# Split-precision projections: high and low activation parts in one 512-column matmul

## The chip, the cores and the metric

The kernel runs on one core of a Trainium2 chip. The metric is device time in microseconds, from the first to the last work of one execution; three timed runs give a median.

## The reference

Two transformer blocks over 256 tokens of 1024 features, float32. Block 1 has two layers, each a SwiGLU feed-forward, a mixer and another SwiGLU feed-forward; block 2 has a mixer of attention and a recurrence, and a convolutional gated feed-forward. Cut to what matters here:

```
def swiglu(h, w_gate, w_up, w_down):          # 1024 -> 2816 -> 1024
    return (jax.nn.silu(h @ w_gate) * (h @ w_up)) @ w_down

for layer in range(2):
    x = x + 0.5 * swiglu(rms_norm(x, ffn1_norm[layer]), ...)
    h = rms_norm(x, mix_norm[layer])
    x = x + (even_mixer(h, ...) if layer == 0 else odd_mixer(h, ...))
    x = x + 0.5 * swiglu(rms_norm(x, ffn2_norm[layer]), ...)
x = rms_norm(x, final_norm)
...                                           # block 2: mixer, gated feed-forward
```

Almost all of the arithmetic is the product of an activation map with a weight matrix.

## The kernel before

**Split products.** Every operand of a projection is split into a high part (rounded to the short float32 format that TensorE takes at full rate) and a low part (the rest). A product is three matmuls into the same place of a PSUM bank: high by high, high weight by low activation, low weight by high activation (`mm3`, lines 301 to 305). The weight tile, 128x128, is the loaded side, and the 256 tokens are the 256 columns that stream. `mm3n` (lines 327 to 331) is the other form, activations loaded and 256 or 512 weight columns streaming; the change leaves it alone.

**Weights.** They come from memory in blocks of 128x1024, eight weight tiles each, on SyncE's queue. `prep` makes the two parts: ScalarE writes `wh` (line 288), VectorE subtracts for `wl` (line 290; some blocks on GpSimd). There are five buffers of each, and `block` keeps six blocks in preparation.

**Activations.** `xh` and `xl` hold eight tiles of 256 tokens, four tiles to a slot of 1024 columns: high parts in two slots, low parts in two others. The feed-forward's inner map (`hh`, `hl`) takes six and six slots for its 22 tiles, the mixers' outputs (`oh`, `ol`) two and two. The pool has 23 slots, given out in turn.

**Stages.** ffn10, mix0, ffn20, ffn11, mix1, ffn21 (block 1), mix2, ffn2 (block 2). A feed-forward of block 1 (`ffn`, lines 450 to 490) runs an up phase over 22 tiles of the inner map: gate block, up block, then VectorE multiplies the gate's bank by the token factor (line 464), ScalarE applies SiLU (466), VectorE multiplies by the up bank (468), and the product is split (469, 470). A down phase follows: 8 output tiles of 22 weight tiles each, then lines 484 and 486, and the next norm's split (`norm_tile`, 383 and 384). The output projections of the mixers are in `out_half`: 8 tiles of four products per half, one VectorE add to `x` each (line 1410 or 1412). In mix2 the second half also makes the split map of the next norm (`def_tile`, 921 and 922), for projections that start before its statistics are known (`def_proj`). `proj_t_steps` serves the query and key projections of mix1 (lines 790 to 806) and mix2 (`main`).

**Order.** The order of the instructions on each engine is set by a scheduler that simulates the program when it is built; the generators only give it the program's order. Banks: four named `mm`, two `sc` (`six_ps` uses all six where attention doesn't), two `aux`.

## Time and profile before

| | us |
|---|---|
| three timed runs | 1420.96, 1419.38, 1416.65; median 1419.38 |
| span of the profiled execution | 1416.2 |
| TensorE, VectorE, ScalarE, GpSimd busy | 1372.7, 942.6, 752.8, 306.0 |

The profiled execution has no time of its own beside its span; the median of the runs is 3.2 us above the span. A matmul's row gives its latency, and matmuls overlap, so what one costs in a stream is the distance between two starts. A weight load (PEld) runs beside the matmul before it. "Idle before, releaser" says how long an engine stood still ahead of an instruction and which instruction ended that.

### The profile page before, as it was taken

To read this page: it belongs to the slowest core of one execution; us is meant where nothing else is said; L and a number is where in the kernel's file an instruction comes from. 1 tells how busy PE (TensorE), PEld (TensorE's weight loads), DVE (VectorE), ACT (ScalarE), POOL (GpSimd) and SP (SyncE) were. 2 spreads that over 40 slices of the span, in tenths; PEclk is the share of its full clock that TensorE was granted. 3 is DMA by queue.
4 is the path that set the end of the run, shared out by engine and by line. 5 is a ranking of instruction groups with operands and counts; after the bars stand their busy time and mean duration, and the time that the engine had idled before them with its cause. 6 is when DMAs were issued, how large, how long until landed. Compare 5 with 4: busy or idle time off the path is not lost.

```text
span 1416.2 us, 26083 instructions
## 1 busy us (share of the span) xinstructions
PE 1372.7 (97%) x10278; PEld 1292.6 (91%) x10278; DVE 942.6 (67%) x1621; ACT 752.8 (53%) x1299; POOL 306.0 (22%) x363
## 2 busy tenths in 40 slices
PE   7999998899999999999999999999989999899997
PEld 6999996579999999999988789999987888799987
DVE  6666656747666656665547766666777778797754
ACT  5444445655444445444467645445557447576642
POOL 4000145423000210000233340000252213741101
PEclk9999999799999999999999999999999999799999
DMA  7655665015555555656565335566546404355561
GB/s 252 190 180 182 185 198 173 8 60 179 181 183 188 180 180 180 188 182 180 186 229 169 101 108 191 181 187 184 180 134 220 132 21 150 118 168 187 182 212 56
DMA packets 64266, 231.70 MB, mean 164 GB/s; under 512 B 7240, under 2 KB 7376, under 8 KB 64144
## 3 DMA queue, kind: packets, MB, share of 16 engines
q1 hardware_dynamic: 61632, 221.41, 49.7%
q0 software_dynamic: 2512, 8.64, 1.7%
q8 instruction: 80, 1.31, 0.4%
q14 instruction: 42, 0.34, 0.1%
HBM read 228.96 MB, written 1.06 MB: 162 GB/s over the span
## 4 chain that ended last, share of the span: by engine, by line
PE 90%; DVE 5%; POOL 2%; ACT 1%; issue 1%; DMA 0%; DVEq 0%; SPq 0%; ACTq 0%
PE mm L303 19%; PE mm L304 18%; PE mm L305 18%; PE sc L304 5%; PE sc L305 5%; PE sc L303 5%; PE mm L331 4%; PE mm L329 4%; PE mm L330 4%; PE mm L549 2%; DVE wl L290 1%; POOL acc L390 1%; PE aux L542 1%; PE sc L518 1%; POOL sq L387 1%
## 5 line engine op out<-in xcount | busy, mean ns | idle before, releaser
L288 ACT ACTIVATE wh<-raw 128x1024 fp32r<-128x1024 f32 (+1 forms) x425 | 443.3, 1045 | 521.3 <-issue 257.3
L290 DVE TENSOR_TENSOR wl<-raw,wh 128x1024 fp32r<-128x1024 f32 (+1 forms) x406 | 510.5, 1260 | 264.8 <-ACT wh L288 263.2
L303 PE MATMUL mm<-xh,wh 128*128 128x256 f32 x1328 | 380.3, 287 | 7.0 <-ACT xh L383 6.0
L304 PE MATMUL mm<-xl,wh 128*128 128x256 f32 x1328 | 380.2, 287 | 3.5 <-DVE xl L384 3.3
L305 PE MATMUL mm<-xh,wl 128*128 128x256 f32 x1328 | 378.5, 285 | 0.3 <-DVE wl L290 0.3
L303 PEld LDWEIGHTS mm<-xh,wh 128*128 128x128 f32 x1328 | 256.7, 194 | 11.0 <-ACT xh L383 6.0
L304 PEld LDWEIGHTS mm<-xl,wh 128*128 128x128 f32 x1328 | 256.6, 193 | 7.3 <-DVE xl L384 5.6
L305 PEld LDWEIGHTS mm<-xh,wl 128*128 128x128 f32 x1328 | 256.8, 193 | 1.4 <-DVE wl L290 0.8
L303 PE MATMUL mm<-hh,wh 128*128 128x256 f32 x704 | 199.2, 283 | 0.0
L304 PE MATMUL mm<-hl,wh 128*128 128x256 f32 x704 | 199.2, 283 | 0.0
L305 PE MATMUL mm<-hh,wl 128*128 128x256 f32 x704 | 199.2, 283 | 0.0
L303 PE MATMUL sc<-xh,wh 128*128 128x256 f32 x560 | 158.7, 284 | 1.9 <-DVE wgb L942 1.9
L304 PE MATMUL sc<-xl,wh 128*128 128x256 f32 x560 | 159.1, 284 | 0.0
L305 PE MATMUL sc<-xh,wl 128*128 128x256 f32 x560 | 158.8, 284 | 0.0
L387 POOL TENSOR_TENSOR sq<-xt 128x256 f32<-128x256 f32 x48 | 36.6, 765 | 514.8 <-DVE xt L486 471.4
L303 PEld LDWEIGHTS mm<-hh,wh 128*128 128x128 f32 x704 | 135.2, 192 | 0.0
L304 PEld LDWEIGHTS mm<-hl,wh 128*128 128x128 f32 x704 | 135.2, 192 | 0.0
L305 PEld LDWEIGHTS mm<-hh,wl 128*128 128x128 f32 x704 | 135.2, 192 | 0.0
L303 PEld LDWEIGHTS sc<-xh,wh 128*128 128x128 f32 x560 | 107.7, 193 | 2.1 <-ACT xt L898 2.1
L305 PEld LDWEIGHTS sc<-xh,wl 128*128 128x128 f32 x560 | 107.7, 192 | 0.1
L304 PEld LDWEIGHTS sc<-xl,wh 128*128 128x128 f32 x560 | 107.6, 192 | 0.1
L331 PE MATMUL mm<-wh,xl 128*128 128x512 f32 x144 | 56.9, 403 | 2.6 <-DVE xl L900 2.6
(345 smaller groups left out, 2265.2 us busy)
## 6 DMA issues: line engine op xcount, KB each, us to landing
raw<-wst SPq DMA_DIRECT2D x417, 512.0 KB, 3.6
m1b<-m1bias POOLq DMA_DIRECT2D x8, 512.0 KB, 4.9
xt<-xT SPq DMA_DIRECT2D x4, 256.0 KB, 5.3
patf<-m2pat POOLq DMA_DIRECT2D x2, 512.0 KB, 6.4
kb<-scr POOLq DMA_DIRECT2D x2, 512.0 KB, 5.9
out<-x2n SPq DMA_DIRECT2D x4, 256.0 KB, 2.0
raw<-wst SPq DMA_DIRECT2D x2, 256.0 KB, 4.2
m0tab<-m0tab POOLq DMA_DIRECT2D x1, 512.0 KB, 3.8
```

Source lines behind the costliest of these rows:

```text
L288: self.nc.scalar.activation(wh[:, c], r[:, c], AF.Copy)
L290: e.tensor_tensor(out=wl[:, c], in0=r[:, c], in1=wh[:, c].bitcast(F32), op=ALU.subtract)
L303: mm(ps, wh, xh, start=first, stop=False)
L304: mm(ps, wh, xl, start=False, stop=False)
L305: mm(ps, wl, xh, start=False, stop=last)
L329: mm(ps, xh, wh, start=first, stop=False)
L330: mm(ps, xh, wl, start=False, stop=False)
L331: mm(ps, xl, wh, start=False, stop=last)
L387: nc.gpsimd.tensor_tensor(out=sq, in0=self.x(j), in1=self.x(j), op=ALU.mult)
L390: self.last_acc = nc.gpsimd.tensor_tensor(out=acc, in0=sq, in1=self.acc, op=ALU.add)
L518: self.nc.tensor.matmul(ps[:, qt], q[own, h, c], low[own], start=False, stop=True)
L549: self.nc.tensor.matmul(po[half * 64:half * 64 + 64, :T], v[kt], pT[:, kt], start=kt == 0, stop=kt == 1)
```

## The change

Each activation tile's high and low parts now lie side by side, 512 columns, two tiles to a slot. `mm2` takes the place of `mm3` where a whole bank is free: one 512-column matmul of the high weight with both parts (high sums in the first half of the bank, low in the second), and one 256-column matmul of the low weight with the high part into the first half. The two halves are then added: `fold` copies the second half out with ScalarE, and VectorE adds the first. The first operation that used the bank before now takes the folded tile. In `out_half` the two halves go to `x` in two VectorE operations; in mix2 the copy was there already, so only an add is new. `ffn2` still passes a slice of 256 columns to `proj_t`, which keeps `mm3` for it; `def_proj` and `mm3n` are as they were. The rest of the diff drops comments and renames.

```
+    def mm2(self, ps, wh, wl, x2, first, last):
+        mm = self.nc.tensor.matmul
+        if first:
+            mm(ps, wh, x2, start=True, stop=False)
+        mm(ps[:, :T], wl, x2[:, :T], start=False, stop=False, skip_group_check=True)
+        if not first:
+            mm(ps, wh, x2, start=False, stop=last)
...
     def proj_t(self, ps):
...
-            self.mm3(ps, wh[:, s], wl[:, s], self.xh(k), self.xl(k), k == 0, k == KD - 1)
+            if ps.shape[1] == 2 * T:
+                self.mm2(ps, wh[:, s], wl[:, s], self.x2(k), k == 0, k == KD - 1)
+            else:
+                self.mm3(ps, wh[:, s], wl[:, s], self.xh(k), self.xl(k), k == 0, k == KD - 1)
...
+    def hi(t, k):
+        return t[k // 2][:, (k % 2) * 2 * T:(k % 2) * 2 * T + T]
+    def lo(t, k):
+        return t[k // 2][:, (k % 2) * 2 * T + T:(k % 2 + 1) * 2 * T]
+    def both(t, k):
+        return t[k // 2][:, (k % 2) * 2 * T:(k % 2 + 1) * 2 * T]
...
     def norm_begin(self):
-        self.xht = [self.slot(f"xh{i}", F32R) for i in range(2)]
-        self.xlt = [self.slot(f"xl{i}", F32R) for i in range(2)]
+        self.xs = [self.slot(f"xs{i}", F32R) for i in range(KD // 2)]
...
     def ffn(self, next_gain):
-        hh = [self.slot(f"hh{i}", F32R) for i in range(6)]
-        hl = [self.slot(f"hl{i}", F32R) for i in range(6)]
+        h2 = [self.slot(f"h{i}", F32R) for i in range(KF // 2)]
...
-            pg = self.six_ps()[:, :T]
+            pg = self.six_ps()
...
-            nc.vector.tensor_tensor(out=s, in0=pg, in1=self.rb, op=ALU.mult)
+            self.fold(s, pg)
+            nc.vector.tensor_tensor(out=s, in0=s, in1=self.rb, op=ALU.mult)
...
-            nc.vector.tensor_tensor(out=hp, in0=pu, in1=sg, op=ALU.mult)
+            self.fold(hp, pu)
+            nc.vector.tensor_tensor(out=hp, in0=hp, in1=sg, op=ALU.mult)
...
-                self.mm3(ps, wh[:, s], wl[:, s], h(hh, k), h(hl, k), k == 0, k == KF - 1)
+                self.mm2(ps, wh[:, s], wl[:, s], self.both(h2, k), k == 0, k == KF - 1)
...
-            nc.vector.scalar_tensor_tensor(out=t, in0=ps, scalar=0.5, in1=self.rb,
+            self.fold(t, ps)
+            nc.vector.scalar_tensor_tensor(out=t, in0=t, scalar=0.5, in1=self.rb,
...
+    def fold(self, out, ps):
+        self.nc.scalar.activation(out, ps[:, T:], AF.Copy)
+        self.nc.vector.tensor_tensor(out=out, in0=ps[:, :T], in1=out, op=ALU.add)
...
     def mix1(self, next_gain):      # qkproj, for q; k in the same way
-                nc.vector.scalar_tensor_tensor(out=q, in0=pq, scalar=0.125, in1=self.rb,
+                self.fold(q, pq)
+                nc.vector.scalar_tensor_tensor(out=q, in0=q, scalar=0.125, in1=self.rb,
...
     def mix2(self, first):          # main
-                nc.scalar.activation(dst[:, t], ps, AF.Copy, scale=sc)
+                nc.scalar.activation(dst[:, t], ps[:, T:], AF.Copy, scale=sc)
+                nc.vector.scalar_tensor_tensor(out=dst[:, t], in0=ps[:, :T], scalar=sc, in1=dst[:, t],
+                                               op0=ALU.mult, op1=ALU.add)
...
     def out_half(self, o2, half, gain, alpha=None, ln=False, six=False):
-                self.mm3(ps, wh[:, s], wl[:, s], oh(4 * half + k), ol(4 * half + k), k == 0, k == 3)
+                self.mm2(ps, wh[:, s], wl[:, s], self.both(o2, 4 * half + k), k == 0, k == 3)
...
-                nc.vector.tensor_tensor(out=x, in0=ps, in1=x, op=ALU.add)
+                nc.vector.tensor_tensor(out=x, in0=ps[:, T:], in1=x, op=ALU.add)
+            nc.vector.tensor_tensor(out=x, in0=ps[:, :T], in1=x, op=ALU.add)
```

What this makes of the instructions, at three places. First TensorE, in the first projection of ffn10: two weight tiles before (`xh`, `xl` are the slots of the high and low parts).

```order
L303 MATMUL mm<-xh_108,wh 128x256
L304 MATMUL mm<-xl_110,wh 128x256
L305 MATMUL mm<-xh_108,wl 128x256
L303 MATMUL mm<-xh_109,wh 128x256
L304 MATMUL mm<-xl_111,wh 128x256
L305 MATMUL mm<-xh_109,wl 128x256
```

And the first three weight tiles now (`xs` holds both parts side by side).

```order
L305 MATMUL mm<-xs_108,wh 128x512
L306 MATMUL mm<-xs_108,wl 128x256 x2
L308 MATMUL mm<-xs_108,wh 128x512
L306 MATMUL mm<-xs_109,wl 128x256
L308 MATMUL mm<-xs_109,wh 128x512
```

Three matmuls per tile have become two, one of them twice as wide, and short and long ones alternate.

Second VectorE, in the up phase of a feed-forward of block 1 (`s` is the gate, `hp` the product, `wl` a weight block's low part). Before, one tile of the inner map:

```order
L464 TENSOR_TENSOR s<-mm,rb 128x256
L290 TENSOR_TENSOR wl<-raw,wh 128x1024
L468 TENSOR_TENSOR hp<-mm,sg 128x256
L290 TENSOR_TENSOR wl<-raw,wh 128x1024
L470 TENSOR_TENSOR hl_186<-hp,hh_180 128x256
```

Now:

```order
L522 TENSOR_TENSOR s<-mm,s 128x256
L496 TENSOR_TENSOR h_5131<-hp,h_5131 128x256
L489 TENSOR_TENSOR s<-s,rb 128x256
L290 TENSOR_TENSOR wl<-raw,wh 128x1024
L522 TENSOR_TENSOR hp<-mm,hp 128x256
L494 TENSOR_TENSOR hp<-hp,sg 128x256
L290 TENSOR_TENSOR wl<-raw,wh 128x1024
```

Two adds (line 522) have come in, each ahead of a weight subtraction; each needs a ScalarE copy of the bank's second half.

Third VectorE, in the second half of mix2's output projection (`dl` is the low part of the next norm's map). Before:

```order
L1412 TENSOR_TENSOR xt<-mm,xt 128x256 x4
L290 TENSOR_TENSOR wl<-raw,wh 128x1024
L922 SCALAR_TENSOR_TENSOR dl_13975<-xt,cols,dh_13972 128x256
L1412 TENSOR_TENSOR xt<-mm,xt 128x256
L290 TENSOR_TENSOR wl<-raw,wh 128x1024
```

Now:

```order
L1440 TENSOR_TENSOR xt<-mm,xt 128x256 x3
L1441 TENSOR_TENSOR xt<-mm,xt 128x256 x3
L290 TENSOR_TENSOR wl<-raw,wh 128x1024
L1440 TENSOR_TENSOR xt<-mm,xt 128x256
L952 SCALAR_TENSOR_TENSOR dl_12017<-xt,cols,dh_12014 128x256
L1440 TENSOR_TENSOR xt<-mm,xt 128x256
L290 TENSOR_TENSOR wl<-raw,wh 128x1024
L1441 TENSOR_TENSOR xt<-mm,xt 128x256
```

Each add to `xt` has become two, in the same queue as the weight subtractions and the splits.

## Rows read from the trace of the kernel before

**Rows 1.** The page: the span, busy time and share of each engine with the number of instructions, and the chain of waits by engine and by line.

```profile
span 1416.2 us, 26083 instructions
...
PE 1372.7 (97%) x10278; PEld 1292.6 (91%) x10278; DVE 942.6 (67%) x1621; ACT 752.8 (53%) x1299; POOL 306.0 (22%) x363
...
PE 90%; DVE 5%; POOL 2%; ACT 1%; issue 1%; DMA 0%; DVEq 0%; SPq 0%; ACTq 0%
PE mm L303 19%; PE mm L304 18%; PE mm L305 18%; PE sc L304 5%; PE sc L305 5%; PE sc L303 5%; PE mm L331 4%; PE mm L329 4%; PE mm L330 4%; PE mm L549 2%; DVE wl L290 1%; POOL acc L390 1%; PE aux L542 1%; PE sc L518 1%; POOL sq L387 1%
```

**Rows 2.** Who waited for whom: total us, times, longest us. One row of ScalarE over the whole span, TensorE's four largest over the whole span, and last TensorE's in the window from 8 to 18 us.

```profile
ACT wh L288 <- PE mm L304: 178.5, 116, 4.1
...
PE sc L515 <- ACT p L525: 6.2, 3, 4.9
PE mm L303 <- ACT xh L383: 6.0, 1, 6.0
PE mm L304 <- DVE dl L922: 5.1, 5, 1.9
PE mm L304 <- DVE xl L384: 3.3, 4, 2.0
...
PE mm L304 <- DVE xl L384: 2.9, 3, 2.0
```

**Rows 3.** TensorE's instructions in order of time, in the up phase of ffn10: start us, latency us. First and last of 25 matmuls of 256 columns that follow one another (24 distances).

```profile
100.06 0.28 PE L303 MATMUL sc<-xh,wh 128*128 128x256 f32 x1
...
102.94 0.28 PE L303 MATMUL mm<-xh,wh 128*128 128x256 f32 x1
```

**Rows 4.** The same view in a projection of mix0: first and last of 17 matmuls of 512 columns (16 distances).

```profile
208.00 0.39 PE L329 MATMUL mm<-wh,xh 128*128 128x512 f32 x1
...
211.63 0.39 PE L330 MATMUL mm<-wl,xh 128*128 128x512 f32 x1
```

**Rows 5.** Groups of TensorE's instructions by line and shape, the first line of `mm3`: count, then busy us and mean latency in ns, then idle time before. `mm` and `sc` are banks; `xh`, `hh`, `oh` the activations' high parts.

```profile
L303 PE MATMUL mm<-xh,wh 128*128 128x256 f32 x1328 | 380.3, 287 | 7.0 <-ACT xh L383 6.0 <-ACT wh L288 0.8 <-ACT xh L899 0.2
L303 PE MATMUL mm<-hh,wh 128*128 128x256 f32 x704 | 199.2, 283 | 0.0
L303 PE MATMUL sc<-xh,wh 128*128 128x256 f32 x560 | 158.7, 284 | 1.9 <-DVE wgb L942 1.9
L303 PE MATMUL mm<-oh,wh 128*128 128x256 f32 x184 | 51.3, 291 | 0.0
L303 PE MATMUL sc<-oh,wh 128*128 128x256 f32 x8 | 2.3, 283 | 0.0
```

**Rows 6.** Durations. Groups by line and shape: ScalarE's weight copy, VectorE's weight subtraction and two products that read a bank (mean ns after the busy us). Last, from the view of one tile, ScalarE's copy of 128x256 out of a bank (min/median/max ns).

```profile
L288 ACT ACTIVATE wh<-raw 128x1024 fp32r<-128x1024 f32 x417 | 441.4, 1059 | 518.4 <-issue 257.3 <-PE mm L304 178.5 <-PE mm L331 54.1
L290 DVE TENSOR_TENSOR wl<-raw,wh 128x1024 fp32r<-128x1024 f32 x398 | 506.5, 1274 | 263.1 <-ACT wh L288 261.5
L468 DVE TENSOR_TENSOR hp<-mm,sg 128x256 f32<-128x256 f32 x59 | 25.0, 424 | 34.6 <-PE mm L305 32.9 <-ACT sg L466 1.7
L1412 DVE TENSOR_TENSOR xt<-mm,xt 128x256 f32<-128x256 f32 x40 | 16.0, 417 | 20.9 <-PE mm L305 20.9
...
L553 ACT ACTIVATE oh<-mm x16: 384/384/388, 266.1 to 831.4; 128x256 fp32r<-128x256 f32 x16
```

**Rows 7.** TensorE's instructions in order of time at the end of block 1, where the granted clock fell: first and last of 11 matmuls of 258 columns (10 distances).

```profile
1041.20 0.42 PE L303 MATMUL mm<-dh,wh 128*128 128x258 f32 x1
...
1043.35 0.42 PE L304 MATMUL mm<-dl,wh 128*128 128x258 f32 x1
```

**Rows 8.** Busy us (and instructions) of each engine by stretch, then granted clock as a share of 2.4 GHz, DMA share, GB/s. The columns: stretch, its length, PE, PEld, DVE, ACT, POOL. Four up phases; a projection of mix0; the query and key projections of mix1 with its attention; the end of mix0's and of mix1's output projection.

```profile
13.00:142.00 129.00, 128.56 (x1042) 127.64 (x1041) 84.44 (x118) 63.64 (x97) 6.84 (x13) 1.00 0.61 193
331.00:460.00 129.00, 128.81 (x1072) 128.55 (x1071) 81.27 (x112) 66.00 (x98) 2.17 (x5) 1.00 0.58 186
524.00:652.00 128.00, 128.00 (x1067) 127.95 (x1067) 81.07 (x113) 64.06 (x94) 1.30 (x4) 1.00 0.60 186
850.00:975.00 125.00, 124.81 (x1039) 124.56 (x1038) 80.09 (x122) 64.78 (x97) 2.31 (x6) 1.00 0.59 185
...
206.60:245.00 38.40, 36.22 (x170) 29.29 (x168) 25.93 (x37) 19.95 (x31) 20.75 (x22) 1.00 0.54 168
...
750.00:815.00 65.00, 65.00 (x409) 51.46 (x408) 49.77 (x137) 43.72 (x111) 21.44 (x19) 1.00 0.38 124
...
320.00:331.00 11.00, 10.95 (x91) 10.75 (x90) 10.39 (x15) 4.54 (x8) 10.53 (x12) 1.00 0.51 162
838.00:850.00 12.00, 11.97 (x100) 11.76 (x99) 11.60 (x17) 5.17 (x8) 11.61 (x12) 1.00 0.52 147
```

**Rows 9.** Instructions in order of time in the second half of mix2's output projection, VectorE's first and last two of 14 rows without a gap, and TensorE's wait at their end.

```profile
1193.06 1.42 DVE L1412 TENSOR_TENSOR xt<-mm,xt 128x256 f32<-128x256 f32 x4 [2.00 <-PE mm L305]
...
1204.27 1.75 DVE L290 TENSOR_TENSOR wl<-raw,wh 128x1024 fp32r<-128x1024 f32 x1
1205.93 1.81 DVE L922 SCALAR_TENSOR_TENSOR dl<-xt,cols,dh 128x256 fp32r<-128x256 f32 x2
...
1206.93 0.58 PE L304 MATMUL mm<-dl,wh 128*128 128x258 f32 x1 [1.68 <-DVE dl L922]
```

**Rows 10.** The same view at the end of block 1: TensorE's wait for the last tile's low part.

```profile
1038.34 0.39 PE L304 MATMUL mm<-dl,wh 128*128 128x258 f32 x1 [0.98 <-DVE dl L922]
```

**Rows 11.** VectorE's instructions in order of time in the up phase of ffn10, one tile of the inner map, with the idle time before each.

```profile
100.26 0.43 DVE L464 TENSOR_TENSOR s<-sc,rb 128x256 f32<-128x256 f32 x1 [0.30 <-PE sc L305]
101.28 1.22 DVE L290 TENSOR_TENSOR wl<-raw,wh 128x1024 fp32r<-128x1024 f32 x1 [0.60 <-ACT wh L288]
103.21 0.42 DVE L468 TENSOR_TENSOR hp<-sc,sg 128x256 f32<-128x256 f32 x1 [0.70 <-PE sc L305]
104.16 1.23 DVE L290 TENSOR_TENSOR wl<-raw,wh 128x1024 fp32r<-128x1024 f32 x1 [0.53 <-ACT wh L288]
105.30 0.42 DVE L470 TENSOR_TENSOR hl<-hp,hh 128x256 fp32r<-128x256 f32 x1
```

More of the change, by code (lines that the diff above doesn't have):

```diff
@@ L701, in mix0 @@
         k_T(SECOND)
-        oh = [self.slot(f"oh{i}", F32R) for i in range(2)]
-        ol = [self.slot(f"ol{i}", F32R) for i in range(2)]
-        OH = lambda t: oh[t // 4][:, (t % 4) * T:(t % 4 + 1) * T]
-        OL = lambda t: ol[t // 4][:, (t % 4) * T:(t % 4 + 1) * T]
+        o2 = [self.slot(f"o{i}", F32R) for i in range(4)]
+        OH, OL = (lambda t: self.hi(o2, t)), (lambda t: self.lo(o2, t))
         def soft_a(i, ps):
@@ L759, in mix0 @@
             n += 1
-        self.interleave(self.out_half(OH, OL, 0, None), att)
+        self.interleave(self.out_half(o2, 0, None), att)
         self.norm_begin()
-        for _ in self.out_half(OH, OL, 1, next_gain):
+        for _ in self.out_half(o2, 1, next_gain):
             pass
@@ L785, in mix1 @@
             load_bias(g)
-        oh = [self.slot(f"oh{i}", F32R) for i in range(2)]
-        ol = [self.slot(f"ol{i}", F32R) for i in range(2)]
-        OH = lambda t: oh[t // 4][:, (t % 4) * T:(t % 4 + 1) * T]
-        OL = lambda t: ol[t // 4][:, (t % 4) * T:(t % 4 + 1) * T]
+        o2 = [self.slot(f"o{i}", F32R) for i in range(4)]
+        OH, OL = (lambda t: self.hi(o2, t)), (lambda t: self.lo(o2, t))
         qk = {}
@@ L836, in mix1 @@
             next(att)
-        self.interleave(self.out_half(OH, OL, 0, None), att)
+        self.interleave(self.out_half(o2, 0, None), att)
         self.norm_begin()
-        for _ in self.out_half(OH, OL, 1, next_gain):
+        for _ in self.out_half(o2, 1, next_gain):
             pass
@@ L1254, in fox @@
                 yield
-        oh = [self.slot(f"oh{i}", F32R) for i in range(2)]
-        ol = [self.slot(f"ol{i}", F32R) for i in range(2)]
-        OH = lambda t: oh[t // 4][:, (t % 4) * T:(t % 4 + 1) * T]
-        OL = lambda t: ol[t // 4][:, (t % 4) * T:(t % 4 + 1) * T]
+        o2 = [self.slot(f"o{i}", F32R) for i in range(4)]
+        OH, OL = (lambda t: self.hi(o2, t)), (lambda t: self.lo(o2, t))
         fox_bias()
@@ L1286, in mix2 @@
         hgrn_end(rr)
-        for _ in self.out_half(OH, OL, 0, None, ALPHA, six=True):
+        for _ in self.out_half(o2, 0, None, ALPHA, six=True):
             pass
@@ L1290, in mix2 @@
         self.def_begin("ln_mix_g", "ln_mix_b")
-        for _ in self.out_half(OH, OL, 1, None, None, True):
+        for _ in self.out_half(o2, 1, None, None, True):
             pass
@@ L1297, in ffn2 @@
         nc = self.nc
-        hh = [self.slot(f"hh{i}", F32R) for i in range(6)]
-        hl = [self.slot(f"hl{i}", F32R) for i in range(6)]
-        h = lambda t, k: t[k // 4][:, (k % 4) * T:(k % 4 + 1) * T]
+        h2 = [self.slot(f"h{i}", F32R) for i in range(KF // 2)]
         x2 = [self.slot(f"x2n{i}") for i in range(2)]
@@ L1321, in ffn2 @@
             nc.gpsimd.tensor_tensor(out=hp, in0=y[0], in1=y[1], op=ALU.mult)
[L1322 to L1323 removed]
+            nc.scalar.activation(self.hi(h2, i), hp, AF.Copy)
+            nc.vector.tensor_tensor(out=self.lo(h2, i), in0=hp, in1=self.hi(h2, i).bitcast(F32), op=ALU.subtract)
             if 8 <= i < 16:
@@ L1390, in proj_t_steps, with out_half @@
             s = slice(k * P, (k + 1) * P)
-            self.mm3(ps, wh[:, s], wl[:, s], self.xh(k), self.xl(k), k == 0, k == KD - 1)
+            self.mm2(ps, wh[:, s], wl[:, s], self.x2(k), k == 0, k == KD - 1)
             if k % 4 == 3:
                 yield
-    def out_half(self, oh, ol, half, gain, alpha=None, ln=False, six=False):
+    def out_half(self, o2, half, gain, alpha=None, ln=False, six=False):
         nc = self.nc
@@ L1398, in out_half @@
         for j in range(KD):
-            ps = (self.six_ps() if six else self.mm_ps())[:, :T]
+            ps = self.six_ps() if six else self.mm_ps()
             for k in range(4):
@@ L1409, in out_half @@
             if alpha is not None:
-                nc.vector.scalar_tensor_tensor(out=x, in0=x, scalar=alpha, in1=ps, op0=ALU.mult, op1=ALU.add)
+                nc.vector.scalar_tensor_tensor(out=x, in0=x, scalar=alpha, in1=ps[:, T:], op0=ALU.mult, op1=ALU.add)
             else:
-                nc.vector.tensor_tensor(out=x, in0=ps, in1=x, op=ALU.add)
+                nc.vector.tensor_tensor(out=x, in0=ps[:, T:], in1=x, op=ALU.add)
+            nc.vector.tensor_tensor(out=x, in0=ps[:, :T], in1=x, op=ALU.add)
             if gain is not None:
```

37 lines of the change are left out of this document (20 added, 17 removed).

## The prediction, made before the changed kernel ran

> **What bounds the kernel now.** I began with the busy shares: TensorE is busy for 97% of the span, VectorE 67%, ScalarE 53% [rows 1]. The chain of waits says that this is no accident of overlap: 90% of the chain that ended last is TensorE's own work, and the three lines of `mm3` lead it [rows 1]. The waits say the same from the other side: the longest totals that TensorE has for any one producer are single microseconds, 6.2, 6.0, 5.1 and 3.3 [rows 2]. So whatever shortens TensorE's stream in the wide stages shortens the kernel, as long as the other engines keep up.
>
> Next, what does one matmul cost in that stream? Not the 283 ns that a row shows (that is its latency), but the distance between starts. In a feed-forward stage 24 starts of 256-column matmuls take 102.94 - 100.06 = 2.88 us, 120.0 ns each [rows 3]. In a projection with 512 columns, 16 starts take 211.63 - 208.00 = 3.63 us, 226.9 ns each [rows 4]. The granted clock is 1.00, the 2.4 GHz level, in both places [rows 8]. 256 columns at 2.4 GHz are 106.7 ns, 512 are 213.3 ns: so each matmul, short or long, carries about 13.3 ns that do not depend on its columns (13.3 from the short ones, 13.6 from the long ones).
>
> **What the change removes.** A weight tile's product now takes one 512-column and one 256-column matmul, 226.9 + 120.0 = 346.9 ns, where it took 3 x 120.0 = 360.0 ns. The columns are the same (768); only one fixed part goes: 13.1 to 13.3 ns, I take 13.3.
>
> How many tiles? The first lines of the triples count 1328 + 704 + 560 + 184 + 8 = 2784 [rows 5]. The last feed-forward stage passes a 256-wide slice and stays with `mm3`: 38 blocks x 8 = 304. Left are 2480: 4 x (44 x 8 + 176) = 2112 in the feed-forward stages of block 1, 16 x 8 = 128 in the odd mixer, 6 x 8 = 48 in the mixer of block 2, 3 x 64 = 192 in the output projections. 2480 x 13.3 ns = **33.0 us** off TensorE's stream, 28.1 of it in the feed-forward stages.
>
> **What it adds, and what covers it.** The two halves of a bank must be added. The folds are 4 x (44 + 8) + 16 = 224, each one ScalarE copy (0.384 us, the row of 128x256 out of a bank) and one VectorE add (0.42 us, as the products out of a bank); six more adds in the mixer of block 2 and 48 in the output projections: 278 x 0.42 = 117 us of VectorE, 224 x 0.384 = 86 us of ScalarE [rows 6].
>
> - Feed-forward, up phase. Four such phases have VectorE at 80 to 84 us of 125 to 129 [rows 8]. 44 adds bring 18.5 us: about 100 of some 123, 81%. ScalarE: 64 to 66 + 44 x 0.384 = 81 to 83. The wait that could spoil this is that the fold stands in VectorE's queue ahead of a weight subtraction. It is covered: ScalarE spends 178.5 us waiting for TensorE to give weight buffers back [rows 2], so conversion runs as far ahead as its five buffers let it. The worst local order is weight copy 1.06, bank copy 0.38, three VectorE operations 1.26, subtraction 1.27: 4.0 us, against four prepared blocks of 2.8 us each, 11 us. Cost 0; if the cover fails the full price is in the third rival.
> - Odd mixer. 16 folds in a stretch where VectorE is busy 49.8 of 65 us and TensorE has no idle time [rows 8]. VectorE has 15 us to spare for 6.7, but scores, softmax and folds now share a queue. Bounds: 0, and all 16 folds exposed, 16 x 0.80 = 12.9 us. I take 2, near the lower end, because the row shows no stall at all today.
> - Output projections ahead of a norm (even and odd mixer). VectorE is busy 10.4 of 11 and 11.6 of 12 us [rows 8], so 8 more adds delay the last low part by up to 8 x 0.42 = 3.4 us each. TensorE does other blocks' early tiles meanwhile (its whole wait for those low parts is 3.3 us, 2.9 of it at the start of the kernel [rows 2]). Bounds 0 and 6.7 together; I take 2.
> - Output projection of block 2's mixer, second half. Here VectorE works without a gap from 1193.06 to 1207.74, and TensorE does wait for it, 1.68 us at the end [rows 9]. Eight more adds lie on this path; four adds in a row took 1.42 us, 0.36 each. Bounds 0 and 3.4; I take 3.0.
> - End of block 1. The last tile's chain runs product, add, split, subtraction, and TensorE waits 0.98 us for it [rows 10]. A copy and an add join it: 0.38 + 0.42 = 0.8.
> - The three other ends of feed-forward stages: TensorE waits nowhere there, the copy and add hide behind seven earlier tiles (7 x 347 ns = 2.4 us). 0; bound 3 x 0.8 = 2.4.
> - Slots: one fewer in each feed-forward stage (11 against 12), no transfer is added. 0.
>
> Sum: -33.0 + 2 + 2 + 3.0 + 0.8 = **-25.2 us**. Against the profiled span, 1416.2 - 25.2 = 1391.0; the median of the runs stands 3.2 us above that span, which I keep: **1394 us**.
>
> **A rule weighed.** The Trainium skill, TensorE: Matmul & The Clock Gate, section Back-to-back issue gap, gives N / 2.4 + 2.5 ns for a warm stream. By it the fixed part is 2.5 ns and not 13.3, the saving is 2480 x 2.5 = 6.2 us, the sum +1.6 us. The trace disagrees: at 120.0 and 226.9 ns both distances lie 11 ns above it. What a smaller fixed part would do here is the second rival.
>
> **The rivals.**
>
> 1. *The adds come out in the mixers.* If the odd mixer and the norms pay near their upper bounds (12.9, 6.7, 3.4, 0.8, 2.4: 26.2 us together), the time is 1416.2 + 3.2 - 33.0 + 26.2 = 1412.6; I let this case cover 1402 to 1413. For it: VectorE at 94 to 97% in two places. Against it: TensorE stalls little there today.
> 2. *No fixed part is saved.* Where the clock fell to 1.2 GHz, ten starts of 258-column matmuls took 2.15 us, 215 ns each, which is 258 columns at 1.2 GHz and nothing over [rows 7]. So the 13.3 ns are not paid under all conditions; if a short matmul between long ones made the long one cost 240 ns, nothing would be gained and the 7.8 us of path cost would stay: 1419.4 + 7.8 = 1427 us. With a third of the 33 us saved it would be 1416. Against it: both lengths show the same remainder at the full clock, with a fresh weight load before each matmul in both. The rule above, from the Trainium skill's page on TensorE, lies between these two ends, at 1421 by its own figure.
> 3. *VectorE becomes the pace of the feed-forward stages (slower).* A pair of blocks now needs two subtractions and five small operations there: 2 x 1.27 + 5 x 0.42 = 4.6 us, of the 5.76 us that a pair takes before. If each fold also stood waiting for a ScalarE copy behind a weight copy, 1.06 + 0.38 = 1.44 us, a pair would take 7.5 us: 88 pairs x 1.8 = +155 us, 1575 us. It decides from 0.55 us of exposed wait per fold upward. For it: today VectorE already waits 0.3 to 0.7 us before its small operations in each pair [rows 11]. Against it: those waits are for TensorE; once VectorE is late, the banks it waits for are long done, and six banks and five weight buffers let TensorE run on.
>
> **How the numbers follow.** Forecast (1385 to 1402): 0.81. Rival 1: 0.10. Rival 2 (1416 to 1427): 0.05. Rival 3: 0.04. Faster by over 0.3% (below 1415.1; less can't be told from no change here) is the first two cases, 0.91; within 0.3% is the milder half of rival 2, 0.03; its other half and rival 3 are slower, 0.06. The range: the lower end is every added cost hidden, 1419.4 - 33.0 = 1386, less one for the spread; the upper end takes in most of rival 1: 1385 to 1410.
>
> **What would show it.** Right: in the feed-forward stages starts at 120 and 227 ns in turn, each of the four stages shorter by about 7 us, VectorE near 80% busy in the up phases and TensorE still without idle time; new TensorE waits in block 2's output projection (about 3 us more) and at the end of block 1. Wrong: a pair of starts that takes 360 ns (rival 2); TensorE waiting for the weights' low part in the up phases (rival 3); or more than 5 us of new idle time in the odd mixer.

## The result: slower, and the profile after

The changed kernel takes **1432.31 us** (median of 4 runs, 1429.62 to 1434.37) against 1419.41 for the kernel before beside it: 0.9% slower, ratio 1.0094 with an interval of 1.0076 to 1.0112. Forecast were 1394 and a range of 1385 to 1410. The profiled execution has a span of 1427.8 us, 11.6 more than before.

The page of the changed kernel, to set beside [rows 1]: span, TensorE's and VectorE's busy time among the engines', and the chain by engine.

```profile
span 1427.8 us, 21874 instructions
PE 1361.7 (95%) x7798; PEld 1160.9 (81%) x7798; DVE 1029.7 (72%) x1899; ACT 816.5 (57%) x1523; POOL 313.4 (22%) x363
PE 85%; DVE 8%; ACT 3%; issue 2%; POOL 1%; DMA 0%; DVEq 0%; SPq 0%; ACTq 0%
```

TensorE's own work falls from 90% to 85% of the chain, and VectorE's and ScalarE's grows from 6% to 11%. TensorE's waits say where, to set beside [rows 2] (us in total, times, longest us):

```profile
PE sc L547 <- ACT p L557: 6.2, 3, 4.9
PE mm L305 <- DVE s L522: 5.4, 3, 2.4
PE sc L549 <- ACT p L557: 5.2, 3, 3.9
PE mm L305 <- DVE xt L1441: 3.4, 4, 1.0
PE aux L456 <- ACT dg L450: 2.4, 2, 1.2
PE sc L305 <- DVE s L522: 2.4, 1, 2.4
```

The first existed before. New are the waits for `s L522`, which is the fold's add (L521 is its copy, on ScalarE), for `xt L1441`, the second add of the output projections, for `dg`, a step of the norm, and 3.9 us for one exponential `p`.

The stream itself did what it should. TensorE in order of time in the up phase of ffn10 (start us, latency us), to set beside [rows 3]:

```profile
102.77 0.40 PE L308 MATMUL mm<-xs,wh 128*128 128x512 f32 x1
103.01 0.28 PE L306 MATMUL mm<-xs,wl 128*128 128x256 f32 x1
103.12 0.39 PE L308 MATMUL mm<-xs,wh 128*128 128x512 f32 x1
...
104.85 0.40 PE L308 MATMUL mm<-xs,wh 128*128 128x512 f32 x1
```

Six pairs of starts take 104.85 - 102.77 = 2.08 us, 346.7 ns each; the forecast was 346.9. Over whole banks of 8 tiles it is a little more: from 60 us on, 28 distances between the first matmuls of successive banks have a mean of 2.797 us, 349.6 ns a tile. Before, a bank took 2.880 us, 360.0 ns a tile. So the gain is 10.4 ns a tile in steady flow, not 13.3.

Where the time went shows only by stage. Boundaries are the first matmul of each stage in the trace; "expected" is the gain of its tiles at 10.4 ns; the last column is what stands against it.

| stage | before | after | expected gain | lost |
|---|---|---|---|---|
| start and ffn10 up | 143.3 | 141.5 | 3.7 | 1.9 |
| ffn10 down, mix0 to its output projection | 137.6 | 139.3 | 1.8 | 3.5 |
| output projection mix0 | 42.7 | 43.7 | 0.7 | 1.7 |
| ffn20, ffn11, ffn21 up | 128.4, 127.6, 128.3 | 128.2, 128.2, 128.3 | 3.7 each | 3.5, 4.3, 3.7 |
| their down phases (ffn11's with mix1's values) | 63.3, 86.2, 63.3 | 61.9, 84.6, 61.8 | 1.8 each | 0.4, 0.2, 0.3 |
| mix1: query, key, attention | 76.6 | 82.4 | 1.3 | 7.1 |
| output projection mix1 | 37.2 | 38.7 | 0.7 | 2.2 |
| end of block 1 and mix2 | 141.0 | 142.7 | 0.5 | 2.2 |
| output projection mix2 | 23.9 | 26.7 | 0.7 | 3.5 |
| last feed-forward | 216.8 | 219.8 | 0 | 3.0 |

The gain is 25.8 us, the losses 37.5: +11.7. (The second row is two stages: the down phase of ffn10 lost 0.4 of the 3.5, mix0 the rest.) The down phases got nearly all of their gain. ffn10's up phase, which loses 1.0 us to one wait for a fold, got half of its own. The three later up phases, with twice the tiles of a down phase, got next to nothing. The windows of ffn20's and ffn11's in the changed kernel (columns as in [rows 8]) show TensorE idle for 3.2 and 2.4 us and the clock at 0.99, where before it was busy to within 0.3 us at 1.00:

```profile
324.50:452.70 128.20, 125.05 (x705) 108.24 (x704) 96.62 (x161) 75.41 (x140) 10.34 (x13) 0.99 0.55 181
514.60:642.80 128.20, 125.80 (x712) 109.35 (x711) 92.17 (x153) 74.35 (x138) 3.27 (x6) 0.99 0.55 181
```

All of that idle time lies in the first 21 us of a phase. TensorE fills its six banks and then needs the first one back. ScalarE's instructions in order of time, 12 to 20 us after the output projection of mix0 ended (324.5), say why it doesn't come:

```profile
336.34 0.24 ACT L436 ACTIVATE nw<-aux,eps 128x2 f32<-128x2 f32 x1
336.50 1.06 ACT L288 ACTIVATE wh<-raw 128x1024 fp32r<-128x1024 f32 x1
337.47 0.19 ACT L437 ACTIVATE nw<-nw 128x2 f32<-128x2 f32 x1
337.56 1.04 ACT L288 ACTIVATE wh<-raw 128x1024 fp32r<-128x1024 f32 x1
338.51 0.19 ACT L438 ACTIVATE nw<-nw 128x2 f32<-128x2 f32 x1
338.60 1.04 ACT L288 ACTIVATE wh<-raw 128x1024 fp32r<-128x1024 f32 x1
341.65 0.69 ACT L450 ACTIVATE dg<-ident,rc 128x128 f32<-128x128 f32 x2 [2.00 <-POOL rc L442]
342.25 1.04 ACT L288 ACTIVATE wh<-raw 128x1024 fp32r<-128x1024 f32 x1
343.20 0.36 ACT L458 ACTIVATE rb<-aux 128x256 f32<-128x256 f32 x1
343.46 0.37 ACT L521 ACTIVATE s<-mm 128x256 f32<-128x256 f32 x1
```

The fold of a bank needs no norm factor. But its copy, the last row, stands in ScalarE's queue behind the whole chain of the norm (`nw`, `dg`, `rb`). TensorE meanwhile waits:

```profile
342.40 0.70 PE L456 MATMUL aux<-dg,ones 128*128 128x256 f32 x2 [1.21 <-ACT dg L450]
345.03 0.76 PE L305 MATMUL mm<-xs,wh 128*128 128x512 f32 x1 [1.93 <-DVE s L522]
```

### The profile page after: what moved, and what is told of

It reads as the page before. It is cut to its first block, busy times and chain, and to the rows that moved or that the text cites. A ratio compares the mean times of both kernels' runs of the same rounds, so it can differ in the third digit from the quotient of the medians.

```text
span 1427.8 us, 21874 instructions
## 1 busy us (share of the span) xinstructions
PE 1361.7 (95%) x7798; PEld 1160.9 (81%) x7798; DVE 1029.7 (72%) x1899; ACT 816.5 (57%) x1523; POOL 313.4 (22%) x363
## 4 chain that ended last, share of the span: by engine, by line
PE 85%; DVE 8%; ACT 3%; issue 2%; POOL 1%; DMA 0%; DVEq 0%; SPq 0%; ACTq 0%
PE mm L308 28%; PE mm L306 16%; PE sc L308 7%; PE sc L306 4%; PE mm L341 3%; PE mm L343 3%; PE mm L342 3%; PE mm L305 3%; PE mm L581 2%; DVE wl L290 2%; PE mm L313 2%; PE mm L312 2%; PE mm L314 2%; ACT wh L288 1%; PE aux L574 1%
## 5 line engine op out<-in xcount | busy, mean ns | idle before, releaser
L308 PE MATMUL mm<-xs,wh 128*128 128x512 f32 x980 | 357.1, 403 | 2.9 <-DVE xs L410 2.9
L306 PE MATMUL mm<-xs,wl 128*128 128x256 f32 x1120 | 294.2, 283 | 0.0
L308 PE MATMUL mm<-h,wh 128*128 128x512 f32 x672 | 237.6, 397 | 0.0
L306 PEld LDWEIGHTS mm<-xs,wl 128*128 128x128 f32 x1120 | 215.2, 192 | 13.2 <-DVE wl L290 0.6
L308 PEld LDWEIGHTS mm<-xs,wh 128*128 128x128 f32 x980 | 186.7, 191 | 43.2 <-DVE xs L410 5.6
L306 PE MATMUL mm<-h,wl 128*128 128x256 f32 x704 | 191.4, 280 | 0.0
L308 PEld LDWEIGHTS mm<-h,wh 128*128 128x128 f32 x672 | 125.9, 188 | 29.0
L308 PE MATMUL sc<-xs,wh 128*128 128x512 f32 x406 | 146.4, 399 | 0.0
L306 PEld LDWEIGHTS mm<-h,wl 128*128 128x128 f32 x704 | 132.9, 189 | 3.1
L306 PE MATMUL sc<-xs,wl 128*128 128x256 f32 x464 | 120.7, 281 | 0.0
L305 PE MATMUL mm<-xs,wh 128*128 128x512 f32 x140 | 58.0, 414 | 13.5 <-DVE xs L410 7.3
L314 PE MATMUL mm<-xs,wl 128*128 128x256 f32 x208 | 59.0, 285 | 0.3 <-DVE wl L290 0.3
```

The lines of the kernel that those rows point to most:

```text
L305: mm(ps, wh, x2, start=True, stop=False)
L306: mm(ps[:, :T], wl, x2[:, :T], start=False, stop=False, skip_group_check=True)
L308: mm(ps, wh, x2, start=False, stop=last)
L314: mm(ps, wl, xh, start=False, stop=last)
```

## The experiments

Two theories at the start. **A:** the matmul gains about what its starts show, and the copy and the adds give it back at a few places: by their position in queues at the starts of the up phases, and in the mixers. **B:** the width gains nothing net, or the clock's low stretches come and go without a cause in the kernel. A diff is against the changed kernel unless said otherwise; every time is a median beside the kernel before on the same chip (1418.7 to 1419.4).

**1. The fold ahead of the norm's chain (first pair of banks of each gated feed-forward).**

```
         self.proj_t(pu)
-        if i == 0:
-            self.norm_end()
         s = self.tmp("s", T)
         self.fold(s, pg)
+        hp = self.tmp("hp", T)
+        self.fold(hp, pu)
+        if i == 0:
+            self.norm_end()
```

> The changed kernel with one thing moved: in the three gated feed-forwards the first gate and up banks are folded (copy and add, before any norm factor is needed) ahead of the norm's chain, not behind it. Theory (the fold copy stands behind the norm chain in ScalarE's queue, so TensorE runs out of its six banks at the start of three up phases, 2.6 to 4.2 us each, and the clock falls to its lower level behind each gap, some 1.7 us each): the waits of TensorE for the folds of these phases are gone and the time falls by 10 to 16 us to 1416 to 1422. Rival A (the wide matmul saves nothing net, the extra copy and add cost it everywhere): same as the change, 1432. Rival B (clock phases that come and go without a cause in the kernel): same time within 3 us, low-clock stretches elsewhere.

1421.61 us, 1.0021 (1.0010 to 1.0032) of before: 10.7 less than the change, inside the theory's range. The up phases take 124.5, 125.2 and 124.0 us, 10.9 us less than in the change. (The two profiled spans differ by 7.1 only: mix0, which the edit doesn't touch, took 2.8 us less, and the last feed-forward 5.3 more (225.1), of which more below.)

**2. The wide matmul in the feed-forwards alone.** The mixers' projections and output projections go back to `mm3` and one read of a bank; one of the four places:

```
-            self.mm2(ps, wh[:, s], wl[:, s], self.x2(k), k == 0, k == KD - 1)
+            self.mm3(ps, wh[:, s], wl[:, s], self.xh(k), self.xl(k), k == 0, k == KD - 1)
```

> The wide matmul and folds in the feed-forwards alone; the mixers' projections and out-projections keep the three 256-column matmuls and their single read of the bank. Theory (the mixers lose 3 + 1 us in mix0, 6 in mix1, 4 in mix2 by the adds and by what they displace): 1432 less 14 to 18, so 1414 to 1419; the odd mixer's first part is back at 99 to 100 us. Rival A (the loss is all in the feed-forwards' starts, the mixers' stretches would come out longer anyway): 1428 to 1433. Rival B (clock phases without a cause): no part of the odd mixer comes back.

1416.59 us, 0.9990 (0.9979 to 1.0001): as the theory had it. The part of mix1 that the table shows at 82.4 is back at 76.7, the output projections at 42.7, 37.1 and 23.9. It shows one thing more: ffn20 and ffn21, which follow an output projection, now take 125.4, but ffn11, which follows a feed-forward with folds, still 128.2.

**3. Both edits together.**

> Both edits together: the wide matmul in the feed-forwards alone, with the first two banks folded ahead of the norm's chain. Theory: the stream saving of the feed-forwards (2112 tiles by about 10 ns, 21 us) shows nearly whole: 1398 to 1406, faster than the kernel before. Rival A (extra copies and adds cost what the matmul saves): 1417 to 1432. Rival B: 1412 to 1420, as the mixers-only edit.

1406.42 us, 0.9927 (0.9906 to 0.9949): just above the theory's range.

**4. The width alone:** three matmuls of 256 columns into the two halves of the bank, folds and order as in the change. (At the start of a bank, not shown, both halves carry a start flag. This kernel leaves out the first tile's product of high by high, but issues every matmul.)

```
...
-            mm(ps, wh, x2, start=False, stop=last)
+            mm(ps[:, :T], wh, x2[:, :T], start=False, stop=False)
+            mm(ps[:, T:], wh, x2[:, T:], start=False, stop=last)
```

> The changed kernel with its folds, halves and buffers, but with the 512-column matmul issued as two of 256 columns into the two halves of the bank. It measures the width alone. Theory (a tile falls from 360 to about 350 ns by the width): 2480 tiles by 10 ns more, 1450 to 1458, the start of each up phase still with its wait. Rival A (the width saves nothing): 1432. A third reading, in which the width saves the 13.3 ns a tile that was forecast and the folds lose the rest: 1462 to 1466.

1436.49 us, only 4.2 more: none of the three. By stage: the down phases are back at 63.3, but the starts of the up phases stall in both kernels, and these phases are only 2.2, 0.4 and 1.2 us longer. mix1's part is 4.0 us shorter (78.4): it waits 1.9 us for the exponential in place of 3.9, for a reason beside the width that the part on mix1 below shows. So this run doesn't weigh the width alone. The test had to be made where nothing waits (run 7).

**5. The last norm's chain unbroken:** one conversion fewer is prepared ahead, and the later ones get an order edge behind the chain's `dg`.

```
-        while self.next_prep < min(self.nblk, b + LOOK):
+        while self.next_prep < min(self.nblk, b + LOOK - self.hold):
...
+            self.hold = 1
             for _ in range(STAT_STEP):
...
             dg = self.bcast_in([m, A], (1.0, -1.0))
+            self.hold = 0
+            self.gate = self.last_dg, self.cur + 8
```

> The changed kernel with one thing about its order: at the layer norm that ends block 2's mixer no weight conversion may stand between the steps of the norm's chain in ScalarE's queue (in the changed kernel a conversion that waits for a weight buffer stands between the first and the second, and another ahead of the last, where the kernel before had none). Theory (TensorE's new waits at the start of the last feed-forward, 4.2 and 1.5 and 1.2 us, come from the chain being 4 us late behind such a conversion): the stretch from the end of mix2's out-projection to the end falls from 219.8 to 214 to 217 us, the time from 1432 to 1426 to 1430. Rival (the chain is late because of the added bank reads of the out-projection, not of the queue): 219 to 220 us, no change of the time.

1431.02 us, and the last stretch takes 220.7: this theory of mine fell. **6.** The same on top of run 3:

> All three edits: the wide matmul in the feed-forwards alone, the first two banks folded ahead of the norm's chain, and the last layer norm's chain unbroken. Theory: the last stretch falls from 224 to 225 us to the 216.8 of the kernel before, so 1406 less 7 to 9, 1396 to 1400. Rival A (the last stretch is long for another reason, a clock phase): 1405 to 1407. Rival B (the late chain costs only what TensorE's waits show, about 4 us): 1401 to 1403.

1405.86 us, 0.9915 (0.9898 to 0.9931): rival A, no gain; the last stretch takes 224.5.

**7. Run 6 with three 256-column matmuls** (the edit of run 4, the second start flag off).

> The same with the 512-column matmul issued as two of 256 columns: folds, banks and order stay. It weighs the width alone where TensorE is not held up elsewhere. Theory (about 9 ns a tile; 2112 tiles less the few at the phases' starts): 15 to 21 us more than with the wide matmul, 1411 to 1421. Rival A (the width itself saves nothing; the gain comes from banks and order): equal within 3 us. Rival C (the 13.3 ns a tile that was forecast): 28 us more, 1424 to 1428.

1424.52 us, 18.7 more, inside the theory's difference of 15 to 21. (The absolute figures on record started from a faster run 6 than was measured, so 1424.5 lies in rival C's range; its difference of 28 does not come.) One up phase, wide first, then narrow:

```profile
321.60:445.60 124.00, 124.00 (x713) 108.16 (x712) 95.58 (x159) 74.80 (x139) 9.48 (x12) 1.00 0.57 191
```

```profile
326.70:455.00 128.30, 128.06 (x1064) 127.59 (x1063) 95.92 (x159) 75.05 (x139) 9.35 (x12) 1.00 0.61 185
```

TensorE is busy throughout in both, and 352 tiles differ by 4.3 us. Over the eight feed-forward phases (each down phase with what follows it to the next boundary) the difference is 20.7 us, 9.8 ns a tile: theory A. (The two profiled spans differ by 16.1: the last stretch is 7.5 shorter in the narrow kernel, mix2 2.9 longer.)

**8. Run 6 with the wide matmul and its adds in the mixers too** (the edit of run 2 undone).

> The same three with the wide matmul and its adds in the mixers too, so that the mixers' part of the change is weighed alone. Theory (odd mixer: a 4 us wait for an exponential behind the added adds, then 10 us at the lower clock, 5 to 6 us in all; the out-projections 1, 1.5 and 2.7 us): 10 to 13 us more than with the feed-forwards alone, 1406 to 1413. Rival (the mixers gain by the stream too once the rest is repaired): equal within 3 us.

1422.15 us, 16.3 more than run 6, worse than the theory's 10 to 13: mix1 82.2 (+5.5), its output projection 40.4 (+3.2), mix2 143.9 (+2.7), its output projection 26.7 (+2.8).

**9. Why the last feed-forward is longer.** In run 6 TensorE waits 4.5 us there, and the rows look like a clash of VectorE and GpSimd: an operation of 0.48 us takes 2.64 while GpSimd converts.

```profile
1231.37 2.71 POOL L293 TENSOR_TENSOR wl<-raw,wh 128x1024 fp32r<-128x1024 f32 x1 [4.39 <-ACT wh L288]
...
1231.33 0.48 DVE L1348 SCALAR_TENSOR_TENSOR s<-dv,cols,s 128x254 f32<-128x254 f32 x1
1231.72 2.64 DVE L1348 SCALAR_TENSOR_TENSOR sg<-dv,cols,sg 128x254 f32<-128x254 f32 x1
```

So that stage's GpSimd conversions went to VectorE, in run 3 (run 9) and, as a control, in the kernel before (run 10).

```
-ON_POOL = {"ffn2": (6, 16, 3), ...
+ON_POOL = {"ffn2": (0, 0, 1), ...
```

> The wide matmul in the feed-forwards alone with the folds ahead (the run of both edits), and in the last feed-forward the four low parts of weights that GpSimd makes go to VectorE instead. Theory (at that feed-forward's start a VectorE operation of 0.48 us takes 2.64 us and two conversions of 1.2 us take 5.05 us while GpSimd converts, the first bank is read 4.5 us late and TensorE stands still): the last stretch falls from 224.4 to 217 to 220 us, the time from 1406 to 1399 to 1402. Rival (VectorE is full there anyway and four conversions more fall on it): the same or longer, 1405 to 1410.

> The kernel before with the same four low parts on VectorE: the control for the run above. Theory (before, no such wait stood there: 216.8 us for the last stretch): within 2 us of the kernel before, 1417 to 1421. Rival (the shared stretch costs the kernel before as much): 1411 to 1414.

1406.76 us and 1419.33 us: the rival for the first, the theory for the second. The wait stays, to the tenth:

```profile
PE mm L312 <- DVE s L1340: 4.5, 1, 4.5
```

The VectorE operation takes 0.48 us again, so the clash is there, but it was not the cause of this wait.

**11. Each fold as one reduction on VectorE,** the rest as in the change.

```
-        self.nc.scalar.activation(out, ps[:, T:], AF.Copy)
-        self.nc.vector.tensor_tensor(out=out, in0=ps[:, :T], in1=out, op=ALU.add)
+        self.nc.vector.tensor_reduce(out=out, in_=ps.rearrange("p (h t) -> p t h", h=2),
+                                     axis=AX.X, op=ALU.add)
```

> The changed kernel with each fold done by one reduction over the two halves on VectorE, so that no copy of a bank stands in ScalarE's queue. Theory (at the starts of the up phases the copy stands behind the norm's chain in ScalarE's queue; VectorE can free the first bank at once): the three stalls of 2.6 to 4.2 us go, as with the folds moved ahead, and the time falls to 1415 to 1423. Rival A (the first bank is late because of the norm factor itself, not of the copy): 1430 to 1434. Rival B (VectorE becomes the pace of the up phases with some 0.2 us more per bank, or as its first product waits for the factor ahead of the second fold): 1432 to 1445.

**1410.09 us**, 0.9945 (0.9929 to 0.9961): 22.2 less than the change by this edit alone, beyond the theory's 1415 to 1423. (Of the 21.7 us between the two profiled spans 2.6 lie in mix0, which has no fold.) Windows of ffn20's and ffn11's up phases and of mix1's part:

```profile
320.40:445.10 124.70, 123.47 (x706) 107.20 (x705) 110.00 (x163) 68.13 (x99) 10.34 (x13) 1.00 0.58 186
507.20:631.80 124.60, 124.25 (x712) 108.12 (x711) 105.87 (x155) 66.82 (x96) 4.19 (x6) 1.00 0.59 186
716.70:791.10 74.40, 74.40 (x386) 56.31 (x384) 64.93 (x155) 52.32 (x121) 26.04 (x22) 1.00 0.49 164
```

The three up phases gain 3.5 to 3.8 us against the change, though VectorE carries 13 us more in each (110.0 for 96.6), and mix1 gains 8.0: it is now 2.2 us shorter than before, so the wide matmul pays there as well. The first bank of ffn20 is folded while the norm's chain still runs, and the product that needs the factor comes 3.3 us later:

```profile
337.09 0.69 DVE L521 TENSOR_REDUCE s<-mm 128x256 f32<-128x512 f32 x1
339.20 1.23 DVE L290 TENSOR_TENSOR wl<-raw,wh 128x1024 fp32r<-128x1024 f32 x1 [1.43 <-ACT wh L288]
340.35 0.42 DVE L489 TENSOR_TENSOR s<-s,rb 128x256 f32<-128x256 f32 x1
```

**12. Run 11 with the output projections back on `mm3` and one read of the bank.**

```
-                self.mm2(ps, wh[:, s], wl[:, s], self.both(o2, 4 * half + k), k == 0, k == 3)
+                self.mm3(ps, wh[:, s], wl[:, s], self.hi(o2, 4 * half + k), self.lo(o2, 4 * half + k), k == 0, k == 3)
...
-                nc.vector.tensor_tensor(out=x, in0=ps[:, T:], in1=x, op=ALU.add)
-            nc.vector.tensor_tensor(out=x, in0=ps[:, :T], in1=x, op=ALU.add)
+                nc.vector.tensor_tensor(out=x, in0=ps, in1=x, op=ALU.add)
```

> The changed kernel with the fold as one reduction on VectorE, and the out-projections back on three 256-column matmuls and one read of the bank. Theory (with the copy gone from ScalarE's queue the wide matmul pays in the odd mixer too, 74.4 us for its first part; what is left of the mixers' loss is the second add of the out-projections: 1, 1 and 2.9 us): 1410 less 4 to 6, 1404 to 1406. Rival (the out-projections' lost time is made up elsewhere): 1409 to 1411.

**1402.35 us**, 0.9880 (0.9864 to 0.9896): the fastest, 7.7 less than run 11. mix2's output projection is back from 26.8 to 23.9, mix0's from 43.5 to 42.7, mix1's from 38.2 to 37.8. That is 4.1 us, as the theory had it; another 3.3 lie in the last feed-forward, which the theory did not have, so the time came out below its range.

**13. Run 12 with order edges at the start of the last feed-forward:** conversions prepared from there on stand behind the third pair's second term.

```
-                nc.scalar.activation(t, ps, AF.Identity, scale=..., bias=...)
+                e = nc.scalar.activation(t, ps, AF.Identity, scale=..., bias=...)
+                if i == 2 and u == 1:
+                    self.gate = e, self.cur + 8
```

> The same with one place of the order held as it was in the kernel before: at the start of the last feed-forward ScalarE makes the third pair's two convolution terms ahead of the next weight conversion, which waits 2.85 us for a buffer (with the change it stands ahead of them). Theory (TensorE's 4.5 us wait there, and the lower clock behind it, come from that one conversion): the last stretch falls from 223 to 225 to 217 to 220 us and the time by 4 to 7, to 1398 to 1401. Rival (the wait comes from the late norm, so another instruction is late next): the time falls by less than 2 us.

1403.36 us: it tells nothing, since run 12's wait at that place was 0.8 us already. **14.** The same edges in run 11, where the wait was 4.5, and for the fourth pair as well (`i in (2, 3)`). ScalarE there before the edit: the row that reads the first bank is the last.

```profile
1226.68 1.06 ACT L288 ACTIVATE wh<-raw 128x1024 fp32r<-128x1024 f32 x1 [1.98 <-PE mm L313]
1227.65 0.59 ACT L1340 ACTIVATE s<-dv,cols 128x256 f32<-128x256 f32 x1
1228.14 0.59 ACT L1340 ACTIVATE sg<-dv,cols 128x256 f32<-128x256 f32 x1
1228.63 1.04 ACT L288 ACTIVATE wh<-raw 128x1024 fp32r<-128x1024 f32 x1
1229.58 0.40 ACT L1349 ACTIVATE h<-hp 128x256 fp32r<-128x256 f32 x1
1229.89 1.99 ACT L288 ACTIVATE wh<-raw 128x1024 fp32r<-128x1024 f32 x2
1231.79 0.40 ACT L1346 ACTIVATE s<-s 128x256 f32<-128x256 f32 x1
1232.09 1.04 ACT L288 ACTIVATE wh<-raw 128x1024 fp32r<-128x1024 f32 x1
1233.04 0.54 ACT L1340 ACTIVATE s<-mm,cols 128x256 f32<-128x256 f32 x1
```

> The changed kernel with the fold as one reduction (1410.1 us, of which the last stretch took 223.1 with a 4.5 us wait of TensorE for the first bank's read), and at that stretch's start two conversions of weights in ScalarE's queue ahead of the first bank's read in place of five. Theory (the read stands behind conversions that wait for weight buffers): the 4.5 us wait is gone or under 1 us, the last stretch takes 217 to 219.5 us, the time 1404 to 1407. Rival (the norm itself is late, the queue's order does not matter): 222 to 224 us, 1409 to 1411.

1404.07 us, 0.9896 (0.9879 to 0.9914): 6.0 less, and the stretch takes 219.3, both as the theory had them. In place of the 4.5 us there is

```profile
PE sc L315 <- DVE s L1350: 0.3, 1, 0.3
```

So conversions that wait at the head of the queue for a weight buffer cost 3.8 us there.

**15. The copy alone:** the kernel before, with each bank of an up phase copied out by ScalarE before VectorE multiplies it (diff against before).

```
-            nc.vector.tensor_tensor(out=s, in0=pg, in1=self.rb, op=ALU.mult)
+            nc.scalar.activation(s, pg, AF.Copy)
+            nc.vector.tensor_tensor(out=s, in0=s, in1=self.rb, op=ALU.mult)
...
```

> The kernel before, with three 256-column matmuls, and in the gated feed-forwards' up phases each bank copied out by ScalarE before VectorE multiplies it: the fold's copy without the width and without the adds before the norms. Theory (the copy costs TensorE something only where the norm's chain is late by more than the six banks cover; before, the factor came 15 us behind the out-projection's end and six banks last 17.3, so 0.4 us of copy fits): 1418 to 1422, up phases 127.5 to 129 us. Rival (a copy in ScalarE's queue stalls TensorE whatever the norm does): the three stalls of the changed kernel, 1427 to 1432.

1418.54 us, 0.9998 (0.9986 to 1.0009): no cost. The window of ffn20's up phase:

```profile
323.90:452.20 128.30, 128.06 (x1065) 127.60 (x1064) 80.66 (x117) 75.06 (x139) 9.18 (x12) 1.00 0.61 185
```

So the copy costs nothing where the chain comes as early as before and the stream is the old one. Starts in us after the end of what precedes the phase, for ffn20 and (in brackets) ffn11; the wait is TensorE's longest for the first bank:

| kernel | `nw`, first step | `rb`, the factor | first bank read from | TensorE waits |
|---|---|---|---|---|
| before | 9.2 (7.8) | 16.6 (13.9) | 17.9 (14.4) | none |
| copy alone (15) | 9.2 (7.8) | 16.6 (13.9) | 16.9 (14.2) | none |
| feed-forwards only (2) | 10.0 (11.0) | 17.5 (18.4) | 17.8 (18.7) | 1.0 (2.4) |
| the change | 11.8 (11.0) | 18.7 (18.5) | 19.0 (18.7) | 1.9 (2.4) |
| reduction (11) | 11.8 (10.0) | 18.6 (17.6) | 16.7 (17.4) | none (0.4) |
| fold ahead (1) | 12.3 (11.5) | 20.7 (20.3) | 10.8 (10.0) | none |

Six banks last 6 x 2.88 = 17.3 us before and 6 x 2.80 = 16.8 with the wide matmul. The norm's own matmuls, some 1.2 us, run in between. In the change the chain starts 2.6 us later for ffn20 and 3.2 for ffn11 (1.7 for ffn21); run 2, without the second add in the output projection, takes back 1.8 of ffn20's 2.6. The faster stream shortens the cover by 0.5, and the fold's add needs another 0.4 us after the copy. Where the bank is read without waiting for the factor, the factor may be later still (run 1: 20.7) and costs no more than 1.1 us at a later bank.

## Why the prediction was wrong

- **The stream (-33.0):** right in kind, too large. The pair takes 346.7 ns inside a bank as forecast, but 349.6 on average, so 2480 tiles give 25.8. Run 7 measured 9.8 ns a tile where next to nothing waits. Rival 2 was wrong. The 2.5 ns of the Trainium skill's formula (TensorE: Matmul & The Clock Gate, Back-to-back issue gap) does not describe this stream either: by this trace 10.4 are saved. The page gives it for matmuls back to back, but that section calls it the gap of an isolated matmul and says that in a stream the weight loads help to set the spacing.
- **Feed-forward, up phase ("Cost 0"): the step that failed.** It set the copy and the adds against ScalarE's 178.5 us of waiting for weight buffers [rows 2] and found cover. But that waiting is no free time in an in-order queue: at a phase's start the copy that frees a bank stands behind the norm's steps, their own waits (2.00 us for GpSimd in the rows above) and the conversions between them. I costed throughput per pair of banks and never asked what the first six banks wait for. The loss is 11.5 us in three up phases and 1.9 in the first; runs 1 and 11 recover 10.9 of the 11.5 by two different edits.
- **Odd mixer (+2, bounds 0 to 12.9):** 7.1 against its own gain, within the bounds, and TensorE's 3.95 us of idle time was nearly the sign I named (over 5). The row that misled was "no stall at all": after 0.65 us of transposes the next matmul in TensorE's queue waits for the exponential.

```profile
755.12 0.65 PE L574 MATMUL aux<-ident,p 128*128 128x128 f32 x4
759.72 0.58 PE L549 MATMUL sc<-qk 128*128 128x256 f32 x1 [3.95 <-ACT p L557]
```

  Run 11 shows that copy and add together do it (one reduction in their place: no wait, 74.4 us). The change's trace shows how part of the 3.95 us comes about:

```profile
755.12 2.34 POOL L290 TENSOR_TENSOR wl<-raw,wh 128x1024 fp32r<-128x1024 f32 x1 [0.66 <-ACT wh L288]
755.62 2.12 DVE L826 SCALAR_TENSOR_TENSOR qT<-qT,rb 128x256 f32<-128x256 f32 x1
757.77 0.85 ACT L529 ACTIVATE qk<-qT 64x256 fp32r<-64x256 f32 x2 [2.46 <-DVE qT L826]
```

  The product with the factor takes 2.12 us while GpSimd converts a weight block, and ScalarE, with the exponential behind in its queue, waits for it. It took 0.42 us in all 16 cases before, where it read the bank, and takes 0.42 us at this place in run 4, which waits 1.9 us. So I put some 1.7 to 2 us of the wait down to this clash, an estimate from 2.12 - 0.42 and 3.95 - 1.9; no run moved the GpSimd conversion at this place, so that is argued, not shown.
- **Output projections ahead of norms (+2):** 3.9 in the two stages themselves, inside the bound of 6.7; and, not in the sum at all, they make the norm late that the next phase waits for (run 2: 1.0 us of waiting for the first bank of ffn20 in place of 1.9).
- **mix2's second half (+3.0):** 2.8 longer, 3.5 with the gain that it should have had, and runs 2 and 12 take it back. Right.
- **End of block 1 (+0.8) and mix2:** 2.2 lost together; run 11 gets 2.1 back.
- **The other ends of feed-forwards (0):** TensorE doesn't wait there, but the statistics come late for the up phase behind (ffn11's brackets above). The bound looked at the wrong end of the chain.
- **The last feed-forward (not in the sum):** none of its own instructions changed, and it took 3.0 us more; 216.7 to 225.2 over all kernels here. Run 14 shows that the order of conversions in ScalarE's queue can cost 3.8 us there; for the change's own 3.0 no run shows the cause (run 5's edit did not shorten it).
- **Rival 1** (the adds come out in the mixers) came in part: 16.7 of the 37.5 us lie in the mixers, their output projections and the end of block 1. The stalls at the starts of the up phases, the other large part, stood in no rival.
- **Rival 3** (VectorE the pace) did not come: run 11 has VectorE at 110 of 125 us and is faster. (Its 88 x 1.8 is 158 us, not 155; nothing hangs on it.)

Seen as a whole: the gain was 7 us smaller than forecast, the costs 37.5 in place of 7.8. Most of that is not the adds' work but the place of copy and add in the queues, as run 11 shows by its 22.2. The 3.1 us of mix0 (77.4 for 74.3) are no cost of the change that a run shows: mix0 has no fold, and runs 3, 6 and 9, whose four engines have the same instructions in the same order up to its output projection, took 82.7, 77.6 and 74.7 us there, at a mean granted clock of 0.79, 0.85 and 0.89. The profile before had 0.89, that of the change 0.85. That much of theory B holds.

## What to carry to other kernels

An instruction that frees a buffer of the bounding engine is to be costed by its place in its engine's queue, at the start of every phase: write down how long the buffers last (here 16.8 us) and what must come first in that queue (here a chain that ends at 18.7 us). An engine's long waiting for something else is no cover, since whatever stands behind the waiting instruction waits too. And a faster stream reaches every old near miss sooner: look for the margins that it uses up before counting its gain.
